# Hybrid decoder trunk: the keys' turning made a step of its own, the bonus raised in VectorE's order, and a wait ahead of the rates

## The chip, the core and the metric

One NeuronCore of a Trainium2 chip runs the whole kernel in one launch. The metric is the device time of an execution in microseconds, as the median of the runs shown. One execution was also taken by the hardware profiler; times in the profile count from its first instruction. Engines: PE (TensorE) with its weight loads PEld, DVE (VectorE), ACT (ScalarE), POOL (GpSimd) and SP (SyncE, which here only issues DMAs).

## What is computed

One decoder layer over 512 tokens of width 2048, all in fp32 (batch 1):

```python
h = rms_norm(x, attn_norm_g)
proj = h @ w_in                      # columns: differential attention, windowed attention, RWKV-7
ya = diff_attention(...)             # 4 heads, causal, ALiBi
yb = sliding_window_attention(...)   # 8 heads, window 128, sinks
yc = rwkv7_time_mix(token_shift(rw)) # 16 heads of 64
x = x + concat(ya, yb, yc) @ w_out
h = rms_norm(x, ffn_norm_g)
x = x + (silu(gate) * up) @ w_down   # gate, up = split(h @ w_gate_up), hidden 5632
out = rms_norm(x, final_norm_g)
```

The change lies in the RWKV-7 part. Per head it runs, over time t,

```python
S = S * w_t + (S @ a_t) b_t^T + v_t k_t^T      # a = -kk, b = kk * iclr, w = decay
y_t = S @ r_t
y = group_norm(y) + sum(r * k * r_k) * v       # the second term is the bonus
```

then multiplies by a gate.

## The kernel before

**Dense work.** Activations lie transposed, features on the 128 partitions and 512 tokens along the free axis. Every large product is done in three fp32r matmuls per 128 x 128 block (high x high, high x low, low x high), accumulated in PSUM: 48 matmuls of 512 columns for a projection of 128 columns. Weights come by SP's DMA in pieces of 512 KB, ScalarE casts the high part, VectorE subtracts for the low one, one projection ahead. `sequence` goes through a list of items: projections k, r, v for each of 8 pairs of RWKV heads, then attention's projections, then the output projection and the FFN.

**Fill-in work.** RWKV and attention run between the dense matmuls. They are Python generators in eight lanes. After every dense matmul `dense_k` calls `pump`, which resumes the generators that are due. What a generator issues up to its next `yield` is a step, and TensorE executes matmuls strictly in the order in which they were issued (`mm` and `tr` keep it), so a matmul whose input or PSUM bank isn't ready holds up all dense work behind it.

**Due times.** The planner keeps a clock of its own: `now` adds up TensorE's work, `charge` books each VectorE and ScalarE instruction by a price (VectorE 0.14 us + 0.00104 us per element) behind what is booked on that engine, and `last` is the end of the step's last booked instruction. After a bare `yield` a lane is due at `last` + 0.3 us (`slack`); after `yield 1.0` at `now` + 1.0; after `yield` of a function when that function says so. A due lane doesn't go at once: it rides when some lane is late by more than 0.4 us, or 1.3 us while a chain runs (`hold`), or when the running chain's own step is due; then all due lanes go together. `need(name)` resumes lanes without dense matmuls in between until the named thing is done.

**Order on the other engines.** VectorE's and ScalarE's instructions are put in order by a scheduler that takes, of what its own reckoning says is ready, the one traced first; `high_priority(300)` places an instruction ahead of up to 300 traced before it. At run time each engine goes through its list in order.

**A pair of heads.** `rates` (lane 4) loads two small weights, makes z and pa on TensorE, two sigmoids, and the scanned decays. It begins when `prep` of the pair before is done. `prep` (lane 0) makes the keys (kn, kk, bk), then Z; then in two groups u of 16 matmuls the products gr, each masked by six VectorE instructions (L586); stores the diagonal blocks for the inverse (li, four DMAs on SP); then turns the keys: eight transposes bt into two PSUM tiles, each copied by ScalarE to bkn (L608). For pairs 2 to 7 the turning waits, where needed, until the chain two pairs back has read its last keys. Then, once that chain's loop is done, vt (v turned, four ScalarE copies to uv, L624), bon (the bonus's row sums) and bv = bon x v on VectorE (L632). The inverse (lane 1, VectorE steps xt and xy, L657 and L658), `join` (px, pt, po), the `chain` over 8 time blocks (z, u, S, y) and `post` (var, g, ysq) follow.

**PSUM.** gr, bt, vt, bon, z, pa and kn all share the tag "m" of pool `pm`, which has two banks. Which bank a tile takes is settled when the program is built.

Of the kernel before, what the change touches and what calls it, by code (L numbers as in the profile page):

```python
# [11 lines left out]
ALU = mybir.AluOpType  # L12
# [76 lines left out]
class Kernel:  # L89
# [389 lines left out]
    def rates(self, hp):  # L479
        nc, rp = self.nc, self.rp  # L480
        q = self.in_flight[hp]
        if hp and f"prep{hp - 1}" not in self.done:
            yield lambda: not (hp and f"prep{hp - 1}" not in self.done)
        if not hp:
            yield 15.0
        ch = slice(hp * P, (hp + 1) * P)
        w2 = rp.tile([97, P], F32, tag="w2", name=f"w2_{hp}", bufs=3)
        a2 = rp.tile([96, P], F32, tag="w2", name=f"a2_{hp}", bufs=3)
        nc.sync.dma_start(out=w2, in_=self.i["w2"][:, ch])
        nc.sync.dma_start(out=a2, in_=self.i["a2"][:, ch])  # L490

        ps = self.pm.tile([P, T], F32, tag="m", name=f"z{hp}")
        self.mm(ps, w2, self.wl)
        sg = rp.tile([P, NCH, 65], F32, tag="rn", name=f"sg{hp}")
        nc.gpsimd.memset(sg[:, :, 0:1], 0.0)

        pa = self.pm.tile([P, T], F32, tag="m", name=f"pa{hp}")
        self.mm(pa, a2, self.al[:96, :], start=True, stop=True)
        a = rp.tile([P, T], F32, tag="a", name=f"a{hp}")
        self.sigmoid(sg[:, :, 1:65], ps.rearrange("p (n c) -> p n c", c=C))  # L500
        self.sigmoid(a, pa, nbias=self.na0[:, hp:hp + 1])
        cum = rp.tile([P, NCH, 65], F32, tag="kk", name=f"cum{hp}")
        nc.vector.tensor_tensor_scan(out=cum.rearrange("p n c -> p (n c)"), data0=self.keep,
                                     data1=sg.rearrange("p n c -> p (n c)"), initial=0.0,
                                     op0=ALU.mult, op1=ALU.add)
        nc.vector.tensor_tensor(out=sg, in0=cum, in1=cum[:, :, 32:33].to_broadcast([P, NCH, 65]), op=ALU.subtract)
        W = rp.tile([P, NCH, 65], F32, tag="W", name=f"W{hp}")
        V = rp.tile([P, NCH, 65], F32, tag="IW", name=f"IW{hp}")
        nc.scalar.activation(W, sg, AF.Exp, scale=-DECAY)
        nc.scalar.activation(V, sg, AF.Exp, scale=DECAY)  # L510
        q["D"] = rp.tile([P, NCH], F32, tag="D", name=f"D{hp}", bufs=3)
        nc.vector.tensor_tensor(out=q["D"][:, 0:NCH - 1], in0=W[:, 0:NCH - 1, 64], in1=V[:, 1:NCH, 0], op=ALU.mult)
        q.update(W=W, V=V, a=a)
        yield

    def prep(self, hp):
        nc, rp = self.nc, self.rp
# [10 lines left out]
        ps = self.pm.tile([P, T], F32, tag="m", name=f"kn{hp}")  # L528
# [44 lines left out]
        for u in range(2):  # L573
            us = slice(4 * u, 4 * u + 4)
            yield
            ps = [self.pm.tile([P, 4, P], F32, tag="m", name=f"gr{hp}_{u}_{h}") for h in range(2)]
# [20 lines left out]
            nc.sync.dma_start(out=d[h, b].rearrange("n s t -> s n t"), in_=L[bl, :, bl])  # L597
        self.done.add(f"r{hp}")
        self.lanes[1].append((f"sub{hp}", self.inverse(q)))

        if hp >= 2 and f"keys{hp - 2}" not in self.done:
            yield lambda: f"keys{hp - 2}" in self.done
        bkn = rp.tile([P, NCH, P], F32, tag="bkn", name=f"bkn{hp}", bufs=2)
        for u in range(2):
            ps = self.pm.tile([P, 4, P], F32, tag="m", name=f"bt{hp}_{u}")
# [9 lines left out]
        v = q["v"]  # L615
        yield
        uv = rp.tile([P, NCH, 2, C], F32, tag="uv", name=f"uv{hp}", bufs=2)
        ps = self.pm.tile([P, 4, P], F32, tag="m", name=f"vt{hp}")
# [10 lines left out]
        ps = self.pm.tile([P, T], F32, tag="m", name=f"bon{hp}")  # L629
        self.mm(ps, rkm, a, start=True, stop=True)  # L630
        bv = rp.tile([P, T], F32, tag="bv", name=f"bv{hp}", bufs=2)
        nc.vector.tensor_tensor(out=bv, in0=ps, in1=v, op=ALU.mult)  # L632
        q["bv"] = bv
        self.done.add(f"v{hp}")

# [679 lines left out]
```

## Time and profile before

| | |
|---|---|
| Three runs, median (lowest to highest) | 2438.54 us (2437.77 to 2443.09) |
| The profiled execution: its own time | 2443.1 us |
| Its span, first to last instruction | 2441.3 us |
| Mean granted clock of TensorE over the span | 0.996 |
| Busy: PE, DVE, ACT | 98%, 49%, 33% of the span |
| RWKV projections (k, r, v of eight pairs) | about 57 to 493 us |
| Attention projections | about 493 to 785 us |
| Output projection, then FFN | 785 to 982 us, then to the end |

"Busy" of TensorE counts pipelined matmuls by modelled ends, so a busy stretch need not be full speed: a dense matmul has a row of 0.39 us but follows the one before by 0.227 us. In the timeline an entry such as [1.49 <-DVE gr L586] is idle time of that engine before the instruction, and what ended it. Granted clock 1.00 is 2.4 GHz, 0.50 is 1.2 GHz.

### The profile page before, as it was taken

The page shows a single profiled execution, that of the slowest core. Times are in us where ns is not written, and L with a number is a line of the kernel's source. Part 1 is how long each engine was busy: PE and PEld are TensorE (multiplying, and loading weights), DVE is VectorE, ACT ScalarE, POOL GpSimd, SP SyncE. Part 2 cuts the span into 40 slices and gives each one's busy share as a digit, 9 for nine tenths or more (in the row PEclk, how much of TensorE's full clock was granted, in tenths as well). Part 3 has the DMA queues.
Part 4 walks back from the last instruction along what each step waited for, and adds up shares of the span by engine and source line. Part 5 has one row for each costly group of instructions (what it writes and reads, how often), then busy time and mean ns, then how long its engine had stood idle before and what let it go on. Part 6 is the DMA issues. An engine that isn't in the chain of part 4 may idle for free.

```text
span 2441.3 us, 30869 instructions
## 1 busy us (share of the span) xinstructions
PE 2403.6 (98%) x12328; PEld 1912.5 (78%) x12328; DVE 1185.9 (49%) x2129; ACT 808.4 (33%) x1375; POOL 99.7 (4%) x158
## 2 busy tenths in 40 slices
PE   8999999999999999999999999999999999999997
PEld 6776676676777778888888888888888888888887
DVE  7577787663545544334343434343434333343437
ACT  5445555534434333322222221222222222222124
POOL 3000000000000003000000000000000000000007
PEclk9999999999999999999999999999999999999999
DMA  5222223232324233322232222322232223232224
GB/s 174 92 86 76 68 85 88 62 91 83 96 95 155 95 124 101 96 96 95 96 100 98 95 95 97 101 96 95 95 101 98 95 95 97 101 97 95 95 100 133
DMA packets 103794, 240.05 MB, mean 98 GB/s; under 512 B 34906, under 2 KB 43746, under 8 KB 103650
## 3 DMA queue, kind: packets, MB, share of 16 engines
q1 hardware_dynamic: 98754, 231.39, 29.6%
q10 hardware_dynamic: 4896, 6.69, 0.8%
q8 instruction: 97, 1.59, 0.3%
q14 instruction: 47, 0.39, 0.0%
HBM read 227.55 MB, written 10.49 MB: 98 GB/s over the span
## 4 chain that ended last, share of the span: by engine, by line
PE 71%; DVE 1%; POOL 0%; issue 0%; ACT 0%; DVEq 0%; ACTq 0%; POOLq 0%
PE pg L134 20%; PE pu L134 20%; PE pd L134 19%; PE po L134 7%; PE pd_qb L134 2%; PE pd_va L134 1%; PE sb L134 0%; PE pd_ka L134 0%; PE ob L134 0%; PE pd_qa L134 0%; POOL acc L1130 0%; PE wtb L138 0%; DVE y L1228 0%; PE oa L134 0%; PE sa L134 0%
## 5 line engine op out<-in xcount | busy, mean ns | idle before, releaser
L134 PE MATMUL pd<-al,wh_wd 128*128 128x512 f32 (+1 forms) x768 | 285.3, 371 | 0.6 <-DVE al L1165 0.6
L134 PE MATMUL pd<-ah,wh_wd 128*128 128x512 f32 (+1 forms) x768 | 285.4, 372 | 0.4 <-DVE y L1184 0.4
L134 PE MATMUL pd<-ah,wl_wd 128*128 128x512 f32 (+1 forms) x768 | 285.2, 371 | 0.0
L134 PE MATMUL pu<-x1h,wh_wu 128*128 128x512 f32 x704 | 274.3, 390 | 0.0
L134 PE MATMUL pu<-x1h,wl_wu 128*128 128x512 f32 x704 | 273.9, 389 | 0.0
L134 PE MATMUL pu<-x1l,wh_wu 128*128 128x512 f32 x704 | 273.9, 389 | 0.0
L134 PE MATMUL pg<-x1h,wl_wg 128*128 128x512 f32 x704 | 273.9, 389 | 0.0
L134 PE MATMUL pg<-x1h,wh_wg 128*128 128x512 f32 x704 | 273.9, 389 | 0.0
L134 PE MATMUL pg<-x1l,wh_wg 128*128 128x512 f32 x704 | 273.9, 389 | 0.0
L1184 DVE TENSOR_TENSOR y<-y,pd 128x512 f32<-128x512 f32 (+1 forms) x192 | 122.5, 641 | 207.8 <-PE pd L134 207.6
L230 ACT CAST wh_wd<-raw_wd 128x1024 fp32r<-128x1024 f32 x96 | 101.0, 1052 | 356.9 <-PE pd L134 177.2
L230 ACT CAST wh_wu<-raw_wu 128x1024 fp32r<-128x1024 f32 x88 | 92.7, 1053 | 367.0 <-PE pu L134 144.7
L230 ACT CAST wh_wg<-raw_wg 128x1024 fp32r<-128x1024 f32 x88 | 92.7, 1054 | 362.5 <-PE pg L134 145.1
L231 DVE TENSOR_TENSOR wl_wg<-raw_wg,wh_wg 128x1024 fp32r<-128x1024 f32 x88 | 107.8, 1225 | 171.1 <-ACT wh_wg L230 171.1
L231 DVE TENSOR_TENSOR wl_wu<-raw_wu,wh_wu 128x1024 fp32r<-128x1024 f32 x88 | 107.8, 1225 | 133.5 <-ACT wh_wu L230 133.5
L134 PEld LDWEIGHTS pd<-al,wh_wd 128*128 128x128 f32 x768 | 144.7, 188 | 25.7 <-DVE al L1165 0.8
L134 PEld LDWEIGHTS pd<-ah,wh_wd 128*128 128x128 f32 x768 | 144.6, 188 | 25.6 <-issue 0.5
L134 PEld LDWEIGHTS pd<-ah,wl_wd 128*128 128x128 f32 x768 | 144.7, 188 | 24.9
L134 PEld LDWEIGHTS pu<-x1l,wh_wu 128*128 128x128 f32 x704 | 132.1, 188 | 27.7 <-issue 0.2
L134 PEld LDWEIGHTS pu<-x1h,wh_wu 128*128 128x128 f32 x704 | 132.1, 188 | 27.7 <-issue 0.2
L134 PEld LDWEIGHTS pg<-x1l,wh_wg 128*128 128x128 f32 x704 | 132.1, 188 | 27.4
L134 PEld LDWEIGHTS pg<-x1h,wl_wg 128*128 128x128 f32 x704 | 132.1, 188 | 27.4
(356 smaller groups left out, 4074.9 us busy)
## 6 DMA issues: line engine op xcount, KB each, us to landing
raw_wd<-in_w_down SPq DMA_DIRECT2D x96, 512.0 KB, 3.2
raw_wg<-in_w_gate SPq DMA_DIRECT2D x88, 512.0 KB, 3.7
raw_wu<-in_w_up SPq DMA_DIRECT2D x88, 512.0 KB, 3.8
raw_wo<-in_w_out SPq DMA_DIRECT2D x32, 512.0 KB, 3.2
raw_k<-in_w_in SPq DMA_DIRECT2D x16, 512.0 KB, 3.8
raw_r<-in_w_in SPq DMA_DIRECT2D x16, 512.0 KB, 3.9
raw_v<-in_w_in SPq DMA_DIRECT2D x16, 512.0 KB, 3.9
x<-in_xT SPq DMA_DIRECT2D x16, 256.0 KB, 4.9
```

Of the source, the lines that this page charges most:

```text
L134: self.tc.keep_in_program_order(self.nc.tensor.matmul(out, lhsT, rhs, start=start, stop=stop))
L230: nc.scalar.copy(out=hi[:, :kn * m], in_=s)
L231: nc.vector.tensor_tensor(out=lo[:, :kn * m], in0=s, in1=hi[:, :kn * m].bitcast(F32), op=ALU.subtract)
L1184: nc.vector.tensor_tensor(out=o, in0=o, in1=ps, op=ALU.add)
```

## The change

Three edits in `rates` and `prep`:

1. `rates` of pairs 1 to 7 waits 1.0 us of planner time after `prep` of the pair before is done. Pair 0 keeps its 15 us.
2. A bare `yield` stands between the masks (with the stores of li) and the turning of the keys. The turning is then a step of its own, due 0.3 us after the planner's end of the last mask.
3. The multiplication bv = bon x v is traced at a priority raised by 300, as other instructions of `prep` are.

```diff
@@ rates @@
         if hp and f"prep{hp - 1}" not in self.done:
             yield lambda: not (hp and f"prep{hp - 1}" not in self.done)
-        if not hp:
-            yield 15.0
+        yield 1.0 if hp else 15.0
         ch = slice(hp * P, (hp + 1) * P)
@@ prep @@
         self.done.add(f"r{hp}")
         self.lanes[1].append((f"sub{hp}", self.inverse(q)))
+        yield
 
         if hp >= 2 and f"keys{hp - 2}" not in self.done:
             yield lambda: f"keys{hp - 2}" in self.done
@@ prep @@
         bv = rp.tile([P, T], F32, tag="bv", name=f"bv{hp}", bufs=2)
-        nc.vector.tensor_tensor(out=bv, in0=ps, in1=v, op=ALU.mult)
+        with self.tc.high_priority(self.lead):
+            nc.vector.tensor_tensor(out=bv, in0=ps, in1=v, op=ALU.mult)
```

## Rows read from the trace of the kernel before

**Rows 1.** The page's busy times (share of span, instructions) and ending chain's shares.

```profile
PE 2403.6 (98%) x12328; PEld 1912.5 (78%) x12328; DVE 1185.9 (49%) x2129; ACT 808.4 (33%) x1375; POOL 99.7 (4%) x158
...
PE 71%; DVE 1%; POOL 0%; issue 0%; ACT 0%; DVEq 0%; ACTq 0%; POOLq 0%
```

**Rows 2.** TensorE's waits, whole span: who <- releaser: us in total, times, longest.

```profile
PE bt L138 <- DVE gr L586: 6.2, 4, 1.7
PE pa L134 <- ACT sg L397: 2.7, 4, 0.7
PE bt L138 <- ACT bkn L608: 2.7, 4, 0.7
```

**Rows 3.** Timeline of PE, pair 0: start, us, instruction, count, [idle before <- releaser].

```profile
100.92 1.16 PE L134 MATMUL gr<-Z,bk 64*128 64x128 f32 x16
103.57 0.63 PE L138 MATMUL bt<-cc,bk 128*128 128x128 f32 x4 [1.49 <-DVE gr L586]
104.88 0.66 PE L138 MATMUL bt<-cc,bk 128*128 128x128 f32 x4 [0.68 <-ACT bkn L608]
```

**Rows 4.** Timeline of DVE, pair 0: first and last of the six masks.

```profile
102.11 0.42 DVE L586 TENSOR_TENSOR linv<-gr,cc 64x256 f32<-64x256 f32 x1 [0.32 <-PE gr L134]
...
104.26 0.41 DVE L586 TENSOR_TENSOR gr<-gr,cc 128x256 f32<-128x256 f32 x1
```

**Rows 5.** Timeline of PE, pair 2: turning of the keys, next dense matmul, next instruction.

```profile
213.68 1.09 PE L138 MATMUL bt<-cc,bk 128*128 128x128 f32 x8
214.52 0.48 PE L134 MATMUL pd_r<-xl,wh_r 128*128 128x512 f32 x1
214.85 0.33 PE L134 MATMUL u<-zs,linv 128*128 128x64 f32 x2
```

**Rows 6.** Stretches: us, busy (instructions) of PE, PEld, DVE, ACT, POOL, clock, DMA.

```profile
102.81:106.23 3.42, 1.98 (x12) 1.64 (x13) 1.78 (x5) 1.17 (x2) 0.00 (x0) 1.00 0.71 191
147.19:150.60 3.41, 1.26 (x15) 1.13 (x16) 3.27 (x9) 0.00 (x0) 0.00 (x0) 1.00 0.26 77
150.60:157.43 6.83, 6.15 (x19) 4.79 (x19) 0.93 (x3) 1.50 (x3) 0.73 (x5) 0.50 0.47 95
...
270.07:273.48 3.41, 3.41 (x9) 1.77 (x8) 0.00 (x0) 1.19 (x2) 0.00 (x0) 0.50 0.33 51
...
509.00:512.42 3.42, 3.42 (x6) 1.35 (x5) 0.09 (x1) 1.84 (x3) 0.00 (x0) 0.50 0.64 131
```

**Rows 7.** Timeline of PE, pair 1: second gr group.

```profile
147.61 0.60 PE L134 MATMUL gr<-Z,bk 64*128 64x128 f32 x6 [0.86 <-DVE gr L586]
```

**Rows 8.** Chain that ended last, in the FFN: start, us, what, matmuls.

```profile
1005.16 10.88 PE pg L134 x48
```

**Rows 9.** Timeline of PE, end of pair 2 and rates of pair 3.

```profile
220.87 1.02 PE L134 MATMUL bon<-a,rkm 128*128 128x512 f32 x2
...
225.36 1.02 PE L134 MATMUL z<-wl,w 97*128 97x512 f32 x2
227.07 1.12 PE L134 MATMUL pa<-al,a 96*128 96x512 f32 x2 [0.69 <-ACT sg L397]
```

**Rows 10.** Timeline of DVE in the same stretch.

```profile
225.22 0.69 DVE L778 TENSOR_TENSOR ysq<-y,ysq 128x512 f32<-128x512 f32 x1 [3.18 <-ACT ysq L774]
...
226.80 0.69 DVE L632 TENSOR_TENSOR bv<-bon,v 128x512 f32<-128x512 f32 x1
```

**Rows 11.** Waits of DVE, 57 to 530 us.

```profile
DVE bv L632 <- PE bon L134: 7.3, 3, 2.9
```

**Rows 12.** Timeline: the first differential head's last VectorE step, and the next projection on PE.

```profile
644.43 0.75 DVE L949 SCALAR_TENSOR_TENSOR osq<-oa,small,osq 128x512 f32<-128x512 f32 x1 [4.72 <-ACT osq L948]
...
650.78 0.39 PE L134 MATMUL pd_ka<-xh,wh_ka 128*128 128x512 f32 x1
```

**Rows 13.** Timeline of PE, pair 4: chain 2's last y matmuls, then vt.

```profile
329.11 0.34 PE L134 MATMUL y<-gr,uv 128*64 128x64 f32 x4
...
331.33 1.05 PE L134 MATMUL vt<-cc,v 128*128 128x128 f32 x8
```

## The prediction

> **What bounds the kernel now.** I read the engine shares first: TensorE is busy 98% of the span, and the chain that ended last is TensorE's for 71% of it [rows 1]. So the time is TensorE's instruction stream plus the moments in which it stands still or runs slowly; what another engine saves counts only where TensorE waited for it. Second, TensorE's own waits [rows 2]: bt, the turning of the keys, waits 6.2 us for the masks and 2.7 us for the copy of its first half, four times each; pa, the second matmul of rates, waits 2.7 us in four places. That is 11.6 us, and all of it lies where the diff cuts. Third, one bt wait from near, in pair 0 [rows 3, 4]. The 16 gr matmuls run from 100.92 to 102.08; bt's first four transposes start at 103.57 after 1.49 us idle, its second four at 104.88 after 0.68 us. Between them VectorE works off six masks of 0.42 us, from 102.11 to 104.67, which read the two "m" banks of gr. bt's first half starts when about three masks have freed the first bank. Its second half does not take the other bank but waits until ScalarE has copied the first half out of the same one. Pairs 1, 3 and 7 are the other three. In pairs 2, 4, 5 and 6 the code already puts bt off until the chain two pairs back is done with its keys; there, in pair 2, all eight run without a gap, 0.84 us from the first transpose (213.68) to the next dense matmul (214.52) [rows 5]. That is bt's price when both banks are free.
>
> Fourth, the granted clock [rows 6]. In the mixer it reads 0.50, the lower of its two levels, in three stretches: 150.60 to 157.43, 270.07 to 273.48 and 509.00 to 512.42. They begin at the end of the bt waits of pairs 1, 3 and 7; behind that of pair 0 it stays at 1.00.
>
> **The step of its own.** Before, bt is issued right behind the second gr group. Now a bare yield stands between. The planner makes the step due at its own estimate of the last mask's end plus 0.3 us, and it forces a ride when 0.4 us late (1.3 us while a chain runs). By the prices in charge a mask is 0.14 + 256 x 0.00104 = 0.41 us; six of them, 0.2 us on, are 2.64 us, so bt leaves some 3.3 us after gr at the earliest, and dense matmuls fill that time. The masks end 104.67 - 102.08 = 2.6 us after gr [rows 3, 4], so 0.7 us of cover are left where VectorE is free. Both banks are then free and the second half's 0.68 us go too, as in [rows 5]. Removed: 6.2 + 2.7 = 8.9 us of idle TensorE [rows 2]. Added: in four pairs TensorE goes over from dense matmuls to fp32 ones and back once more. The nearest row for that is 214.52 to 214.85, 0.33 us for the first dense matmul behind bt [rows 5], against a pitch of 10.88 / 48 = 0.227 us [rows 8]: 0.1 us, and I count as much for the way in, 0.8 us in four pairs; it is nothing where the step rides with another lane's. Moved: two ScalarE copies, and with them vt, bon and the next pair's rates, by some 3 us in these four pairs. The step issues no DMA, the stores of li stay ahead of it, and it is moved past nothing on SP or POOL. What comes late by it is the next pair's preparation, not a dense matmul.
>
> **The clock.** At the lower level TensorE was busy 6.15 + 3.41 + 3.42 = 13.0 us [rows 6]; at the higher one this is half, so 6.5 us were lost. All three stretches begin on bt waits, and I count them as gone. The lower bound is nothing, if the falls have another cause; as no row shows a fall in the mixer without a bt wait, I take the upper end.
>
> The Trainium skill (TensorE: Matmul & The Clock Gate, Part 1, What's actually happening) says that the monitor behind this clock runs freely and does not restart with a kernel. By that rule the same wait can be followed by a fall in one execution and not in the next; pair 0's row agrees. By the rows alone every execution of before would lose the 6.5 us and gain 17.0 us by this change; by the rule one with no fall would gain 10.5 us.
>
> **Rates and the bonus.** In pair 2 bon starts at 220.87; z of the next rates starts at 225.36, and pa waits 0.69 us until ScalarE has read z out of the same bank, because the other bank still holds bon [rows 9]. VectorE had stood idle for 3.18 us ahead of ysq, whose input comes from ScalarE, and did bv only at 226.80, though bon's matmul was over by about 222 [rows 10]. Raised, bv stands ahead of ysq in VectorE's order and frees the bank some 4 us earlier; no work is added, 0.69 us of VectorE are moved. Rates in turn wait 1.0 us more, and for a ride on top of it, so that bv can be done before z is issued. Either is enough for pa to find a bank of its own: 2.7 us go [rows 2]. Cost: z and pa no longer ride with var and g; as a burst of their own they cost at most 0.2 us in four pairs, 0.8 us, and nothing on a chain's step. I take 0.4. The two loads that rates issues on SP move with it, behind whatever weights SP has queued by then; before, no wait of TensorE for z's or pa's weights stands among its waits [rows 2], so I take 0 for them. Queued behind the raised bv on VectorE are masks, inverse steps and weight splits; should bon be late, they wait with it. In three pairs VectorE already waits for bon, 7.3 us in all and at most 2.9 us at a time [rows 11], and TensorE waits in none of them. I take 0, and keep -0.5 to +2.9 us for the range.
>
> **The sum.** The profiled execution took 2443.1 us, 1.8 us over its span of 2441.3. 8.9 + 6.5 + 2.7 = 18.1 us go, 0.8 + 0.4 = 1.2 us come: 16.9 us, 2426.2 us, say 2426. The profiled execution is the slowest of the three shown, 4.6 us over the median of 2438.5. I read this as falls of the clock that the others had less of and that the changed kernel has not at all, so the number stands against the median as well (12.5 us, 0.5%). If it is slower for a reason that stays, the median comes to 2421.5.
>
> **Rivals.** (a) *The clock falls anyway*, behind other waits, as that of gr itself in pair 1, 0.86 us [rows 7]. Then 6.5 us stay: 2432.7. Against it: no such place shows a fall of its own before.
> (b) *The wait comes back at the new place.* The due time rests on the planner's book of VectorE. In pair 1 VectorE was busy 3.27 of 3.41 us ahead of the fall [rows 6], and gr had waited for it as well [rows 7]. If VectorE runs behind its book by more than the 0.7 us of cover in all four pairs, bt waits again, the clock falls again, and pa's 2.7 us alone are won: 2440.4. Against it: in pair 0 the six masks follow each other closely [rows 4], and the inverse's steps are in the book too.
> (c) *The change does not do what it says*: bv keeps its place in VectorE's order because its input becomes ready too late in the scheduler's reckoning. The rates' wait covers most of that; at worst 2.7 us are missing, 2428.9, inside the main case.
> (d) *Slower: the rates' wait adds up along the pairs.* The rates of a pair start when prep of the pair before is done, and prep needs its rates. If this ring set the pace, pair 7 would be late by 7 x (1.0 + 1.3) + 4 x 3 = 28 us. That meets the end of attention's third qa projection (h = 2), where the code issues without dense work until the first differential head is done: the next projection begins at 650.78, the head's last VectorE step ends at 645.2 [rows 12], 5.6 us of room. 28 - 5.6 = 22 us of idle TensorE against 16.9 won: 2448.6. It decides from a lateness of some 22 us. Against it: in pairs 2, 4, 5 and 6 vt waits for the chain, in pair 4 vt comes 2.2 us behind the last y matmul of chain 2 [rows 13], so what such a pair had lost before is taken in there. I expect 3 to 6 us of lateness at the end.
>
> **How the numbers follow.** About 0.2%, 4.9 us, is what a measurement of this kernel can tell from no change; faster is below 2433.7 us. Main case with (c): 0.66, 2420 to 2431. Better than that, because the profile's 4.6 us stay and gr's 0.86 us go as well: 0.06, 2419 to 2420. (a): 0.12, 2430 to 2436, half of it faster. (b): 0.10, 2435 to 2441, same. (d): 0.06, slower. Faster 0.78, same 0.16, slower 0.06. The range holds the main case and the better one, all of (a) and the start of (b): 2419 to 2437.
>
> **What would show it.** In the profile after: eight transposes without idle in every pair, with dense matmuls between the second gr group and bt; no bt and no pa in TensorE's waits; a clock of 1.00 through the mixer; bv within about 1 us of bon's end in each pair; the FFN unchanged at 10.88 us for 48 matmuls. The prediction is wrong if bt still waits for masks (b), if the clock reads 0.50 behind other waits (a), or if the attention projections show idle that was not there (d).

## The result

| | median (lowest to highest) | profiled execution: own time, span |
|---|---|---|
| before | 2438.46 us (2437.77 to 2443.09), six runs | 2443.1 us, 2441.3 us |
| after | 2425.02 us (2423.44 to 2425.95), six runs | 2425.95 us, 2424.2 us |

The ratio is 0.9939, with a 95% interval of 0.9927 to 0.9950: 0.6% faster. The two medians in the table lie 13.4 us apart. The forecast was 2426.0 us, between 2419 and 2437. From profile to profile the span is 17.1 us shorter, and all of it is there when the output projection begins; the FFN only starts earlier. The parts are read in the order of the prediction.

The page of the changed kernel, busy times: us, share of the span, instructions. It answers to [rows 1]; TensorE is busy 5 us less in a span 17 us shorter.

```profile
PE 2398.7 (99%) x12328; PEld 1912.3 (79%) x12328; DVE 1185.3 (49%) x2129; ACT 806.4 (33%) x1375; POOL 100.0 (4%) x158
```

The longest waits of TensorE in the changed kernel over the span: who <- releaser: us in total, times, longest. They answer to [rows 2]; the four left out are 0.8 us or less each and have neither bt nor pa among them.

```profile
PE pd_l L134 <- ACT hl L333: 7.4, 2, 6.1
PE gr L134 <- DVE gr L585: 1.6, 2, 0.8
PE wt L138 <- DVE pa L906: 1.3, 2, 0.9
...
```

bt and pa are gone from the list, so 8.9 and 2.7 us of idle are won. gr is longer, 1.6 us against 0.86 [rows 7]: it is the one wait left where the change cuts.

Timeline of the changed kernel, pair 0, first TensorE and then VectorE's first and last mask: start, us, instruction, count. They answer to [rows 3, 4].

```profile
100.95 1.16 PE L134 MATMUL gr<-Z,bk 64*128 64x128 f32 x16
...
105.57 0.39 PE L134 MATMUL pd_k<-xh,wh_k 128*128 128x512 f32 x1
105.81 1.04 PE L138 MATMUL bt<-cc,bk 128*128 128x128 f32 x8
106.60 0.48 PE L134 MATMUL pd_k<-xl,wh_k 128*128 128x512 f32 x1
```

```profile
102.14 0.42 DVE L585 TENSOR_TENSOR linv<-gr,cc 64x256 f32<-64x256 f32 x1 [0.32 <-PE gr L134]
...
104.28 0.41 DVE L585 TENSOR_TENSOR gr<-gr,cc 128x256 f32<-128x256 f32 x1
```

Dense matmuls without idle fill the time between gr and bt, the last mask ends at 104.69, and the eight transposes go in one piece from 105.81 to the next dense matmul at 106.60. No pair has a wait of bt in the list any more. The cover is thin in pair 2, though: there bt starts at 209.47, before the last mask has ended at 210.00.

The same kernel, pair 1: TensorE's second gr group, and two stretches of 3.41 us (columns as in [rows 6]).

```profile
147.21 0.46 PE L134 MATMUL gr<-Z,bk 64*128 64x128 f32 x2 [0.81 <-DVE gr L585]
148.43 1.13 PE L134 MATMUL gr<-Z,bk 64*128 64x128 f32 x14 [0.77 <-DVE gr L585]
```

```profile
146.34:149.75 3.41, 1.84 (x18) 1.53 (x18) 3.30 (x8) 1.01 (x2) 0.00 (x0) 1.00 0.19 30
149.75:153.16 3.41, 3.41 (x9) 2.67 (x9) 3.29 (x8) 0.00 (x0) 0.83 (x6) 0.50 0.62 169
```

Here the clock still falls, behind gr's waits and not behind bt's; it is the mixer's only stretch at 0.50, 3.41 us where there had been 13.65. The FFN is unchanged at 10.88 us for 48 matmuls [rows 8].

Rates, in the changed kernel: TensorE at the end of pair 2 (to set beside [rows 9]), and VectorE around bv in pairs 2 and 3 (beside [rows 10]).

```profile
214.27 1.02 PE L134 MATMUL bon<-a,rkm 128*128 128x512 f32 x2
...
217.41 1.02 PE L134 MATMUL z<-wl,w 97*128 97x512 f32 x2
218.27 1.02 PE L134 MATMUL pa<-al,a 96*128 96x512 f32 x2
```

```profile
215.33 0.69 DVE L633 TENSOR_TENSOR bv<-bon,v 128x512 f32<-128x512 f32 x1 [2.30 <-PE bon L134]
...
276.91 0.75 DVE L781 SCALAR_TENSOR_TENSOR ysq<-ysq,cols,bv 128x512 f32<-128x512 f32 x1
277.77 0.69 DVE L633 TENSOR_TENSOR bv<-bon,v 128x512 f32<-128x512 f32 x1
```

In pair 2 bv comes at once. In pair 3 bon ends at 272.9 and bv starts 4.9 us later, as late as in any pair before, although it is raised; pairs 4 and 6 show the same. So the raise does not do what the prediction took it to do. No run leaves the raise out of the changed kernel; that it does nothing there is read from these three pairs and from e3 below.

### The profile page after: what moved, and what is told of

Read it like the earlier page. It is cut to its first block, busy times and chain, and to the rows that moved or that the text cites. A ratio compares the mean times of both kernels' runs of the same rounds, so it can differ in the third digit from the quotient of the medians.

```text
span 2424.2 us, 30859 instructions
## 1 busy us (share of the span) xinstructions
PE 2398.7 (99%) x12328; PEld 1912.3 (79%) x12328; DVE 1185.3 (49%) x2129; ACT 806.4 (33%) x1375; POOL 100.0 (4%) x158
## 4 chain that ended last, share of the span: by engine, by line
PE 92%; DVE 4%; DMA 1%; issue 1%; ACT 1%; POOL 0%; SPq 0%; DVEq 0%; ACTq 0%; POOLq 0%
PE pg L134 20%; PE pu L134 20%; PE pd L134 19%; PE po L134 8%; PE pd_r L134 3%; PE pd_v L134 3%; PE pd_k L134 2%; PE pd_ka L134 2%; PE pd_qa L134 2%; PE pd_va L134 2%; PE pd_qb L134 2%; PE pd_l L134 1%; PE z L134 1%; PE y L134 1%; DVE xy L659 1%
## 5 line engine op out<-in xcount | busy, mean ns | idle before, releaser
L134 PEld LDWEIGHTS pu<-x1h,wl_wu 128*128 128x128 f32 x704 | 132.1, 188 | 27.5
```

Source lines behind the costliest of these rows:

```text
L134: self.tc.keep_in_program_order(self.nc.tensor.matmul(out, lhsT, rhs, start=start, stop=stop))
```

## Experiments

### Each edit alone

Turning as a step of its own, on the kernel before:

```diff
         self.lanes[1].append((f"sub{hp}", self.inverse(q)))
+        yield
```

> The kernel before with the yield ahead of the keys' turning alone. Theory A (the sum of the prediction: this step carries the gain): bt's 8.9 us of waits go and, with them, the clock falls that followed them; 8.9 + 4.8 to 6.5 - 0.8, so 12.9 to 14.6 us faster than before on the profile's own time, about 2424 to 2430 us; pa's four waits of 0.69 us stay. Rival B (the rates' wait or the raise carries it, the step only trades places): under 5 us faster.

Measured: 2429.83 us (2428.99 to 2432.16), ratio 0.9954 [0.9941, 0.9966]. TensorE's waits in this kernel that bear on it, and its clock around 612 us:

```profile
PE pa L134 <- ACT sg L397: 3.4, 5, 0.7
PE wt L138 <- DVE st L904: 3.0, 1, 3.0
PE gr L134 <- DVE gr L586: 1.5, 2, 0.8
...
611.69:615.10 3.41, 2.96 (x11) 2.71 (x12) 1.61 (x4) 0.48 (x1) 0.00 (x0) 0.50 0.18 65
```

bt is gone, pa stays, and gr takes 1.5 us as in the full change: gr's longer wait comes with this edit. The clock falls once, here behind a wait of attention's wt. This edit carries three quarters of the gain (0.46% of 0.61%). The 12.9 to 14.6 us that were expected stood against the profile of before, and 2443.1 - 2428.99 = 14.1 us meets them; from median to median it is 10.2 us.

The rates' wait alone:

```diff
-        if not hp:
-            yield 15.0
+        yield 1.0 if hp else 15.0
```

> The kernel before with the rates' 1.0 us wait alone. Theory A: pa finds a bank of its own, 2.7 us of waits go, bt's waits and the clock falls stay as they are: 2 to 3 us faster than before, 2435 to 2437 us, which is inside what counts as the same. Rival B: 5 us or more. A third reading, that a delay of the rates alone shifts the lanes so that bt waits in other pairs: bt's waits differ from 8.9 us by a pair's 2.2 us either way.

Measured: 2444.32 us (2437.40 to 2447.52), ratio 1.0012 [1.0004, 1.0021]: not faster. TensorE's waits:

```profile
PE bt L138 <- DVE gr L585: 8.1, 5, 2.5
PE bt L138 <- ACT bkn L607: 3.4, 5, 0.7
...
PE px L134 <- DMA linv<-xi: 1.0, 2, 0.7
```

pa's 2.7 us are gone, so this edit does by itself what the prediction wanted of it. But the pairs stand otherwise against the chains, five of them instead of four now meet their masks, and the mixer has five stretches of 3.41 us at 0.50. What it wins, the turning loses again, and the rest of the loss is clock: ten of the eleven executions have a mean granted clock of 0.993 to 0.996 and take 2442.63 us or more, while the only one at 0.998 took 2437.40 us, no longer than before. Next to e1 the same line, together with the raise, is worth 0.9939 / 0.9954, another 0.15%, 3.7 us. The two intervals overlap, but the profiled spans differ by 3.0 us. So the value of an edit depends on whether the other is there.

The raise alone:

```diff
-        nc.vector.tensor_tensor(out=bv, in0=ps, in1=v, op=ALU.mult)
+        with self.tc.high_priority(self.lead): nc.vector.tensor_tensor(out=bv, in0=ps, in1=v, op=ALU.mult)
```

> The kernel before with bv's raised priority alone. The prediction's reading (bv stands behind ysq because of the order alone): bv runs within 1 us of bon's end in all pairs, pa's 2.7 us go. Rival, from the trace of after, where bv of pairs 3, 4 and 6 still runs right behind L781's read of the bonus two pairs back: bv waits for its own output buffer, of which there are two, so the raise moves nothing; the time is that of before within 0.1% and bv stands behind ysq in pairs 2, 4, 5 and 6 as before.

Measured: 2439.84 us (2437.79 to 2443.97), ratio 0.9997 [0.9987, 1.0006]. In the two traces every engine runs its instructions in the same order with the raise as without it, and TensorE's waits from 57 us to the FFN are those of before. This kernel's pa wait, VectorE around bv in pair 2, and the mixer's only stretch at 0.50:

```profile
PE pa L134 <- ACT sg L397: 2.7, 4, 0.7
...
224.44 0.75 DVE L780 SCALAR_TENSOR_TENSOR ysq<-ysq,cols,bv 128x512 f32<-128x512 f32 x1
...
225.30 0.69 DVE L632 TENSOR_TENSOR bv<-bon,v 128x512 f32<-128x512 f32 x1
...
151.58:154.99 3.41, 3.41 (x11) 2.82 (x12) 0.00 (x0) 0.59 (x1) 0.73 (x5) 0.50 0.39 60
```

Two things follow. The raise moves nothing. And since it moves nothing, this is a second profile of the program before, by chance one with less low clock: 3.41 us in the mixer in place of 13.65 [rows 6], at the same waits, and a span of 2436.4 us in place of 2441.3. Of these 4.8 us, 0.3 are there before the first RWKV projection begins (57.06 us as against 57.38). The other 4.5 us, for 10.24 us of low clock, 0.44 us each, are the price of the falls alone, and they account for nearly all of the 4.6 us by which the profile of before lay over its median.

### Why bv is late

In the kernel before, between the rows of [rows 10], stands this line of VectorE's timeline:

```profile
225.95 0.75 DVE L780 SCALAR_TENSOR_TENSOR ysq<-ysq,cols,bv 128x512 f32<-128x512 f32 x1
```

It reads the bonus of the pair two back, and bv starts as it ends. The tag "bv" has two buffers, so the third bonus needs the buffer of the first. If that is the cause, a third buffer does what the raise does not. Kernel before, with three (the tag's other users, in attention, take the new count, and the pool of raw weights goes from three buffers to two for the room):

```diff
-        bv = rp.tile([P, T], F32, tag="bv", name=f"bv{hp}", bufs=2)
+        bv = rp.tile([P, T], F32, tag="bv", name=f"bv{hp}", bufs=3)
```

> The kernel before with three buffers in place of two for the bonus bv (and, to make room in SBUF, two in place of three for the raw weights, which may cost time of its own, so only the rows around bon, bv and pa count). Buffer theory: bv runs within 1 us of bon's end in pairs 2, 4, 5 and 6, where it ran 4 to 5 us behind it, and pa's four waits of 0.69 us go. Order theory: bv stays behind ysq and pa waits as before.

Measured: 2436.52 us in one execution, span 2434.7 us; one execution compares no times, so only the rows count. bon and bv of pair 2 and of pair 5 in this kernel's timeline, and the wait that is left where it matters:

```profile
220.73 1.02 PE L134 MATMUL bon<-a,rkm 128*128 128x512 f32 x2
221.79 0.69 DVE L632 TENSOR_TENSOR bv<-bon,v 128x512 f32<-128x512 f32 x1 [0.50 <-PE bon L134]
...
397.25 1.02 PE L134 MATMUL bon<-a,rkm 128*128 128x512 f32 x2
398.63 0.69 DVE L632 TENSOR_TENSOR bv<-bon,v 128x512 f32<-128x512 f32 x1
...
PE bt L138 <- DVE gr L586: 6.2, 4, 1.7
```

bv follows bon within 0.4 us in all eight pairs, in pair 5 ahead of the read of the older bonus (405.16 us in the kernel before, 401.99 us here), and pa no longer waits; bt is as it was. So pa's wait has two cures, the buffer and the rates' wait, and the raise is neither.

### Is it the split or the due time?

The changed kernel with the step due at `now` + 0.5 in place of the planner's end of the masks:

```diff
-        yield
+        yield 0.5
```

> The changed kernel with the keys' turning due 0.5 us after the second gr group in place of the planner's end of the masks. Theory A (it is the due time at the masks' end that saves, not the step of its own): bt leaves some 0.9 us after gr, the masks take 2.6 us, so bt waits again, 0.5 to 1.5 us in each of pairs 0, 1, 3 and 7 and 0.7 us for its second half, with falls of the clock: 5 to 9 us over the changed kernel, 2430 to 2434 us. Rival (the split alone is enough): within 1 us of the changed kernel.

Measured: 2437.67 us (2436.22 to 2439.41), ratio 0.9988 [0.9979, 0.9997]. TensorE's waits:

```profile
PE bt L138 <- ACT bkn L608: 2.7, 4, 0.7
PE bt L138 <- DVE gr L585: 2.1, 4, 1.0
...
PE gr L134 <- DVE xt L658: 1.8, 1, 1.8
PE px L134 <- DMA linv<-xi: 1.8, 3, 0.7
```

A step of its own that comes too early wins next to nothing: the transposes stand before masks again, the second half behind its copy again, four times each, and other products begin to wait. The gain hangs on the due time. This is rival (b) made to happen, at 2437.7 us where it was put at 2440.4.

### What one bt wait costs in the changed kernel

The changed kernel without the new step in pair 3 was meant to price a single wait:

> The changed kernel, but in pair 3 alone the keys are turned right behind the masks again. Theory A (each wait costs its idle time and, in some executions, a fall of the clock behind it): bt waits 1.49 + 0.68 us in pair 3 and nowhere else; 2.2 us over the changed kernel where the clock holds, 3.9 us where it falls, so 2427 to 2429 us. Rival: the wait is filled from later idle time, within 0.5 us of the changed kernel.

Measured: 2424.29 us (2423.97 to 2425.30), ratio 0.9930 [0.9918, 0.9943], and no bt wait at all. In the changed kernel the chains lie so that pair 3's turning already waits for the keys of the chain two back. The run says that much and prices nothing. Pair 7 was not run without the step; there chain 5's last product with its keys starts at 499.98 and the masks end at 501.51, so whether it depends on the step is open. Pairs 0 and 1 have no chain to wait for, so the step was taken from them:

```diff
-        yield
+        if hp > 1:
+            yield
```

> The changed kernel without the yield in pairs 0 and 1, the two pairs whose turning no other condition now holds back. Theory (a bt wait costs its idle time, and a fall of the clock where one follows): pair 0's bt waits return, 1.49 + 0.68 us, and pair 1's, about 1.7 + 0.7 us; idle of TensorE before the FFN up by some 4.5 us from 3.8, less what the extra changes between dense and fp32 matmuls cost (0.4 us). The clock reads 0.50 behind pair 1 for 3.4 to 6.8 us as against 3.4 in the changed kernel, so up to 1.7 us more: 2429 to 2431 us. Rival (the waits are only passed on to the next product behind, which then waits less): the time stays within 1.5 us of the changed kernel's, 2424 to 2426.5.

Measured: 2431.02 us (2428.82 to 2432.04), ratio 0.9961 [0.9949, 0.9974], against 0.9939 of the changed kernel: 0.22%, 5.4 us. TensorE in pair 1:

```profile
152.34 0.63 PE L138 MATMUL bt<-cc,bk 128*128 128x128 f32 x4 [2.50 <-DVE gr L585]
153.65 1.11 PE L138 MATMUL bt<-cc,bk 128*128 128x128 f32 x4 [0.68 <-ACT bkn L609]
```

With pair 0's 1.49 and 0.68 that is 5.4 us of bt waits, gr's 1.6 us gone and the whole idle of TensorE between 57 us and the FFN up from 3.8 to 8.0 us. The profiled spans differ by 2.9 us, 3.4 us from the first RWKV projection on, with as much low clock in either. So the waits cost time and aren't just handed on, as the theory had it, at the upper end of its forecast. The profiled execution is the shortest of the five, at a mean granted clock of 0.998; the other four, at 0.996 to 0.997, took 1.0 to 3.2 us longer. So the median's further distance goes with a lower clock than the profile has.

### gr's wait and the last fall

The changed kernel with pair 1's second gr group 2.0 us later:

```diff
-            yield
+            yield self.last + self.slack - self.now + (2.0 if u and hp == 1 else 0.0)
```

> The changed kernel with the second gr group of pair 1 due 2.0 us later. In the changed kernel's profile this group is the only place of the RWKV stretch where TensorE still waits for masks (0.81 + 0.77 us), and the only one behind which the clock reads 0.50 (3.41 us). Theory A: both go, 1.6 + 1.7 us, 2421 to 2423 us. Rival (the lanes shift by 2 us and meet VectorE's work elsewhere): a wait of about the same size at another place, within 1 us of the changed kernel.

Measured: 2423.74 us (2423.30 to 2425.07), ratio 0.9927 [0.9914, 0.9941]: no difference to the changed kernel that could be told. gr's waits are gone, and in their place in this kernel's pair 1, with a fall of 3.41 us from 156.40:

```profile
154.55 0.96 PE L134 MATMUL px<-cc,linv 32*32 32x32 f32 x32 [1.47 <-DMA linv<-xi]
...
156.40:159.81 3.41, 3.41 (x40) 2.41 (x39) 0.00 (x0) 1.04 (x3) 0.00 (x0) 0.50 0.95 272
```

The wait has moved to px, the inverse's first product, which needs two DMAs through DRAM. Put off both:

```diff
+            yield self.last + self.slack - self.now + (2.0 if u and hp == 1 else 0.0)
...
-        yield 10.0
+        yield 13.0
```

> The changed kernel with pair 1's second gr group put off by 2.0 us of planner time, and with the inverse's first product px asked for 13.0 us of planner time behind its loads in place of 10.0, in every pair. Theory (each wait is a step that is due too early, and there is room behind it): gr's 1.6 us and px's 1.47 us both go, and with them the fall of the clock behind them, 1.7 us: about 3.3 us less than the changed kernel, 2421 to 2422.5 us. Rival (in pair 1 VectorE is simply full, so a wait that is put off shows up at the next product or lengthens the ring of preparations): some other wait of 1 to 2 us shows up in pair 1, a fall of the clock stays, and the time is 2423 to 2426 us.

Measured: 2421.05 us (2420.45 to 2421.24), ratio 0.9921 [0.9908, 0.9935], span 2418.7 us: faster than both kernels, 4.0 us below the changed one. What is left of TensorE's waits between 57 us and the FFN, and the mean clock of 57 to 980 us:

```profile
PE S L134 <- ACT uv L743: 1.2, 1, 1.2
PE z L134 <- DVE uv L756: 0.9, 1, 0.9
PE oss L134 <- ACT osq L944: 0.7, 1, 0.7
...
57.00:980.00 923.00, 920.10 (x5673) 686.65 (x5672) 567.51 (x1418) 434.53 (x935) 35.20 (x82) 1.00 0.30 95
```

No stretch of the mixer is at 0.50. With the last fall gone, its four executions lie within 0.8 us of each other, where those of before lie 5 us apart. The two intervals overlap, but the profiled spans differ by 5.5 us, 5.0 of them between the first RWKV projection and the FFN. Of these the idle explains 0.9 (3.8 to 2.9 us) and the fall 1.5 by e3's price; the other 2.6 us aren't explained. px was put off in all eight pairs, and no run puts it off in pair 1 alone.

### How far the rates may wait

The changed kernel with 6.0 in place of 1.0, to call up rival (d):

```diff
-        yield 1.0 if hp else 15.0
+        yield 6.0 if hp else 15.0
```

> The changed kernel with the rates waiting 6.0 us in place of 1.0. Theory A (the ring of rates and prep does not set the pace; the chain two pairs back does): within 4 us of the changed kernel, no idle time in the attention projections beyond the 1.3 us that it has there, the last pair's chain ends at most 10 us later. Rival (d) of the prediction (the wait adds up along seven pairs): 7 x 5 = 35 us more lateness at the last pair, over 20 us of idle TensorE where attention needs the chain: 2445 us or more.

Measured: 2452.15 us (2450.22 to 2454.08), ratio 1.0043 [1.0030, 1.0057]: slower than before. Its longest wait in TensorE's list, attention's wait, VectorE's last inverse step with SP's store and load in pair 1, and the clock behind it:

```profile
PE px L134 <- DMA linv<-xi: 16.0, 4, 7.5
...
PE oss L134 <- ACT osq L944: 0.5, 1, 0.5
...
146.46 0.17 DVE L659 TENSOR_TENSOR xy<-xy,xt 128x8 f32<-128x8 f32 x1
146.71 2.60 SPq L663 DMA_DIRECT2D xi<-xy  x4
150.78 1.82 SPq L674 DMA_DIRECT2D linv<-xi  x4
153.91 1.25 PE L134 MATMUL px<-cc,linv 32*32 32x32 f32 x32 [3.83 <-DMA linv<-xi]
...
154.31:167.96 13.65, 13.65 (x134) 10.90 (x131) 3.67 (x7) 4.40 (x9) 0.00 (x0) 0.50 0.15 33
```

The size is that of rival (d), 2448.6 us, but not the place: attention waits 0.5 us, px 16.0 us for the inverse's way through DRAM. If that is the cause, px asked for later takes it away:

```diff
-        yield 1.0 if hp else 15.0
+        yield 6.0 if hp else 15.0
...
-        yield 10.0
+        yield 20.0
```

> The changed kernel with the rates' wait at 6.0, as in the run before it with that wait, and px asked for 20.0 us of planner time behind the inverse's loads in place of 10.0. Theory (the run with 6.0 alone lost its time because the late preparation shifted px to where its loads from DRAM had not landed: 16 us of idle for the loads and then falls of the clock): px's waits for the loads go, the low clock falls from 34 us to at most 10, and the time is 2425 to 2433 us. Rival (the loads' waits are a by-product; the ring of preparations is simply longer and meets the chain or attention): the idle time moves to other products (S, gr, osq) and the time stays above 2440 us.

Measured: 2433.46 us (2431.95 to 2435.64), ratio 0.9975 [0.9965, 0.9984]. The two longest waits between 57 us and the FFN:

```profile
PE S L134 <- ACT uv L743: 3.0, 3, 1.2
PE var L134 <- ACT ysq L770: 1.8, 1, 1.8
```

px waits nowhere, the low clock of the mixer and attention is 3.41 us in place of 34.13, and 18.7 us are back. So px's DMA was most of the loss. 8 us over the changed kernel are left. 8.3 us of idle in all between 57 us and the FFN, as against 3.8, now lie at the chain's products and at attention's, as in the rival's account. Some of the other 4 us go with the clock: e12's profile is its shortest execution, and its ten have a mean granted clock of 0.996 to 0.997, those of the changed kernel 0.997 to 0.998. How much it is wasn't followed up.

## Why the prediction was right, and where it was not

**The turning: right in place and size.** All 8.9 us of bt's idle went, and dense matmuls cover the masks, as the sum says. The yield alone (e1) and the yield with another due time (e9) show that the due time does it. One term was missing: in two halves the transposes also run longer. The dense matmul behind bt's second half in pair 0 of before, to set beside [rows 3]:

```profile
105.29 0.47 PE L134 MATMUL pd_k<-xh,wh_k 128*128 128x512 f32 x1
```

From 103.57 to 105.29 are 1.72 us, 1.04 without the idle; in one piece it is 0.79 us. Four pairs like it give 1.0 us more than the sum had. Against it stand 1.2 us counted for new bursts of fp32 work among the dense matmuls, of which the trace shows eight more; no run prices them.

**The clock: right in sign, too large.** 6.5 us were booked on the ground that every fall stood behind a bt wait. By e3's price the 10.24 us of low clock that went were worth 4.5 us. 3.41 us stayed, where the prediction had named a clock of 0.50 behind other waits as a sign of being wrong: this is rival (a) in small, the fall moved behind gr, whose wait grew by 0.7 us. The prediction had the row [rows 7] and took it as too short to count. That gr waits longer comes with the step in pairs 0 and 1 (e10 takes it out there, and gr's wait is gone); why it does is not shown. e7 and e11 show that the wait and the fall can be put off by due times.

**Rates and bonus: right sum, wrong cause.** The 2.7 us went, but not by the raise. The step that failed is "Raised, bv stands ahead of ysq in VectorE's order and frees the bank some 4 us earlier": it took the order for the cause. The row between those of [rows 10] (L780, above) shows what bv really waits for, its own buffer; e3 and e4 settle it. Rival (c) came true for a reason it didn't name, and cost nothing, where it had allowed up to 2.7 us, because the rates' wait covers it (e2). "Either is enough" was wrong for one of the two. The rates' wait was also given a price without looking at what it does to the pairs' places: alone it brings more bt waits and more falls of the clock (e2).

**The sum.** 8.9 of bt, 4.5 of clock, 2.7 of pa, 1.0 of the turning itself and 0.4 of wt against 0.7 of gr make 16.8 us; the span is 17.1 us shorter, and 16.9 had been booked. Without the clock the check is cleaner: e3's profile has the waits of before and the same 3.41 us of low clock as the changed kernel, and from the first RWKV projection to the FFN the changed kernel is 12.6 us shorter than it; the terms without the clock make 12.3. So 2 us of error in the clock were made good by a term that was missing and by new bursts that left no cost to be seen in these sums, though 1.2 us had been booked for them. That is luck; the agreement to 1 us is better than the reasoning.

**The median.** The prediction read the profile's 4.6 us over the median as falls which other executions had less of. e3 is such an execution: same order of instructions, same waits, 10.24 us less of low clock, 4.8 us less span. The 51 executions of before that were taken beside the experiments say the same: the 13 with a mean granted clock of 0.998 took 2437.97 to 2438.80 us, the eight at 0.994 to 0.995 took 2441.38 to 2445.34 us. So the median of 2438.46 us, inside the first group, held few falls, and the 13.4 us from median to median are nearly all waits and turning. The rule of the Trainium skill that the prediction weighed (TensorE: Matmul & The Clock Gate, Part 1, What's actually happening), that the clock's monitor runs freely and doesn't restart with a kernel, agrees with these two profiles: the same waits were followed by three falls in one and by one in the other.

**Rival (d).** At 1.0 us it did not come: attention's list shows no new wait. At 6.0 us a loss of its size came, but the prediction had its bound in the wrong place. It counted rates' own two loads on SP and did not look at the inverse's stores and loads, while those set how early px may stand in TensorE's order (e12).

## What to carry to other kernels

On an engine that bounds the kernel and works in strict order, a short step that needs another engine's result belongs at that engine's expected end, not behind the step that feeds it; a plain split doesn't do it. Before an instruction is raised because it comes late, look for the reader of the buffer it writes: a late writer behind that reader needs a buffer, not a priority. When one wait is put off, look at once at the step next in line, and put off both; and measure edits together as well as alone, since here one made the kernel 0.12% slower alone, by falls of the clock, and about 0.15% faster beside the other.

## What the hardware showed that was not expected

- The same order of instructions with the same waits had 13.65 us of the mixer at half clock in one profile and 3.41 us in another; 10.24 us of it cost 4.5 us. Pair 0's waits of 1.49 and 0.68 us were followed by a fall in none of before, e3 and e10, while pair 1 had one in each of them.
- A fall is not tied to one kind of wait: it came behind bt, behind gr (changed kernel), behind px's 1.47 us (e7) and behind attention's wt, 2.99 us (e1).
- The way of the inverse through DRAM took 7.4 us from VectorE's last step to the first product (146.46 to 153.91 us in e8), for four small stores and four small loads, more than half of it from the stores' issue at 146.71 to the loads' at 150.78.
